# The first mixer's two attention loops: maxima ahead of the last unit's scale, values a step later, weight splits over two steps

## The chip, the cores and the metric

One core of one Trainium2 chip runs the whole kernel. The metric is the device time of one execution in microseconds (us). The core has five engines with a queue each: TensorE (PE) for matrix products and transposes, VectorE (DVE) and ScalarE (ACT) for work on elements, GpSimd (POOL), and SyncE (SP), which issues most of the transfers. Each queue is worked off in its order, and engines wait for one another through semaphores.

## What is computed

A trunk of two layers on 512 rows of 1024 numbers. The change lies in the attention part of the first layer, which has two kinds of heads behind one input projection; the rest (the gated feed-forward blocks and the second layer's attention) is not touched.

```python
def mla_attention(q_nope, q_rope, k_nope, k_rope, v):      # 8 heads
    s = (einsum(qn, k_nope) + einsum(qr, k_rope)) * scale  # 128 queries at a time
    s = where(kpos <= qpos, s, -inf)
    return einsum(softmax(s), v)

def diff_attention(q1, q2, k1, k2, v, lam, slopes):        # 4 heads
    p = softmax(q1 @ k1 * scale + bias) - lam * softmax(q2 @ k2 * scale + bias)
    return einsum(p, v)

o_mla = mla_attention(...)
o_diff = rms_norm(diff_attention(...), subln_g) * (1.0 - lam_init)
return concatenate([heads_last(o_mla), heads_last(o_diff)], -1) @ w_out
```

## The kernel before

The 512 rows are worked on as four tiles of 128. A product with weights is made of three matmuls (`mm3`, lines 263 to 265): every operand is split into a high part, rounded by a cast on ACT (`wh`, L72), and a low part, the difference, by a subtraction on DVE (`wl`, L73). `Weights` holds a list of weight units of 128x1024 numbers. `load` issues a unit's transfer into one of three raw buffers, `ahead(n)` casts and subtracts up to unit n, and `next` hands out the next unit.

The first attention (functions `m_...`) has 32 units: eight heads, in pairs, with four query tiles each. Unit i of a head has (i+1)*128 columns. A unit goes through these operations: the score product on PE into one of two banks (L776); the row maximum on DVE (L594, `softmax_negated`, which works on negated scores and also adds the mask); the exponential on ACT with its row sum (L596); reciprocal and scale on DVE (L782, L783, `m_scale`); the transposes on PE, i+1 of them (L793, `m_turn`); and the copy of the transposed weights out of the bank by DVE (L804) or, in the odd head, ACT (L802). After eight units the value product of a pair of heads follows (L811, `m_values`), and its split.

The second attention (functions `d_...`) has 16 units, four heads with query tiles 3, 2, 1, 0. A unit has two scores and two softmaxes (L674, L594, L596), a combination of the two on DVE (`d_combine`: reciprocals and products, L683 to L686), transposes (L868) and their copy (L870), the value product (L880), a scale by the first sum (L882), a square sum on ACT (L884), the root on POOL (`rstd`), and the norm on DVE (L890). After a head's four units `d_finish` transposes the head's output (L895) and splits it into `oD`, named odh and odl in the profile.

Between the steps of both loops PE gets other matmuls (`Fill`): the projections of values (`diff_v`, tile av) and of queries and keys (`diff_qk`, tile aqk) of the second attention, then the first half of the output product (`project`, tile ao). These are generators, and one call of `fill(n)` takes n pieces. Before, a piece is an `mm3`, so three matmuls.

Both loops stand in a manual schedule: the order in which the code issues the instructions is the order of each queue. In step n of the first loop the code issues the scale of unit n-1, the transposes and the copy of unit n-2, the score and the maximum of unit n, then one piece of filling. In step m of the second loop it issues the norm of unit m-3, the combination of m-1, the transposes and copy of m-2, scores and maxima of m, filling, the value product of m-2, and filling. In steps named in the table `made`, the cast and the subtraction of a weight unit follow at the end of the step.

The tiles that set limits: `s` (the weights of a unit) has four buffers, of which a unit of the second attention takes two; the banks of the matrix results are named a (three), s (two), t, o and n (one each). The first attention's transposes use t and n in turn, the second's use t.

Behind the loops come the second half of the output product, the residual and the first feed-forward block, in an order that is the same in both kernels.

Of the kernel before, what the change touches and what calls it, by code (L numbers as in the profile page):

```python
# [17 lines left out]
P = 128  # L18
# [68 lines left out]
def trunk(tc, A, out):  # L87
# [3 lines left out]
    with ExitStack() as top:  # L91
# [481 lines left out]
        def even():  # L573
            with ExitStack() as es:
# [24 lines left out]

                def diff_qk(h, z):  # L600
                    acc = bank("a", "aqk")
                    wh, wl = W.next()
                    for k in range(KD):
                        if k:
                            yield
                        mm3(acc, wh[:, k * P:(k + 1) * P], wl[:, k * P:(k + 1) * P],
                            xh[:, k], xl[:, k], k == 0, k == KD - 1)
                    if z == 0:
                        ACT.activation(dq[h], acc, AF.Copy, scale=-0.125)
                    else:  # L610
                        DVE.tensor_copy(dk[h], acc)

                def diff_v(tiles):
                    accs = [bank("a", "av") for _ in tiles]
                    for k in range(KD):
                        wh, wl = wv[k // 2]
                        c = slice((k % 2) * 512, (k % 2 + 1) * 512)
                        for a, i in zip(accs, tiles):
                            if k or i != tiles[0]:
                                yield  # L620
                            t = slice(i * P, (i + 1) * P)
                            mm3(a, xh[:, k, t], xl[:, k, t], wh[:, c], wl[:, c], k == 0, k == KD - 1)
# [3 lines left out]
                class Fill:  # L626
# [9 lines left out]
                    def end(self):  # L636
                        self(1000)

# [24 lines left out]
                otoks, dens, d_s, d_pt, d_r = {}, {}, {}, {}, {}  # L663
                D_UNITS = [(h, i) for h in range(4) for i in ORDER]

                def d_score(m):
                    h, i = D_UNITS[m]
                    w = (i + 1) * P
                    if i == ORDER[0]:
                        dens[h] = sx.tile([P, 6, NT], F32, tag="den", name="den", bufs=2)  # L670
                    s_ps = [bank("s", "sps") for _ in range(2)]
                    for z in range(2):
                        r = slice(z * 64, (z + 1) * 64)
                        PE.matmul(s_ps[z][:, :w], dq[h][r, i * P:(i + 1) * P], dk[h][r, :w], start=True, stop=True)  # L674
                    d_s[m] = [softmax_negated(s_ps[z][:, :w], alibi[h // 2][:, h % 2, 384 - i * P:], w)
                              for z in (1, 0)]

                def d_combine(m):
                    h, i = D_UNITS[m]
                    w = (i + 1) * P  # L680
                    (s2, st2), (s1, st1) = d_s[m]
                    v = dens[h][:, :, i:i + 1]
                    DVE.reciprocal(v[:, 0], st2[:, 1:2])  # L683
                    DVE.scalar_tensor_tensor(v[:, 1], v[:, 0], st1[:, 1:2], neglam[0], ALU.mult, ALU.mult)
                    DVE.scalar_tensor_tensor(s1[:, :w], s2[:, :w], v[:, 1], s1[:, :w], ALU.mult, ALU.add)
                    DVE.reciprocal(v[:, 2], st1[:, 1:2])  # L686
                    d_s[m] = s1

                with ExitStack() as e1:
# [82 lines left out]
                    def m_score(n):  # L772
                        p2, i, z = M_UNITS[n]
                        h, w = 2 * p2 + z, (i + 1) * P
                        s_ps = bank("s", "sps")
                        PE.matmul(s_ps[:, :w], mq[h][:, i * P:(i + 1) * P], mk[h][:, :w], start=True, stop=True)  # L776
                        m_s[n] = softmax_negated(s_ps[:, :w], dv[:, 0, 384 - i * P:], w)
# [7 lines left out]
                    def m_turn(n):  # L785
# [4 lines left out]
                        pt = pts[p2, z]  # L790
                        tp = bank("tn"[z], "tpp", 4, P)
                        for j in range(i + 1):
                            PE.transpose(tp[:, j], s[:, j * P:(j + 1) * P], ident[:])  # L793
                        for j in range(0, i + 1, 2):
# [23 lines left out]
                    made = {2: 14, 21: 15, 25: 16, 29: 17}  # L818
                    fill = Fill(diff_v((3, 2)), diff_v((1, 0)), *[diff_qk(h, z) for h in range(1, 4) for z in range(2)])
                    o = None  # L820
                    with tc.manual_schedule(engines=everything):
                        for n in range(M + 2):
                            if n + 2 in made:
                                W.load()
# [38 lines left out]
                def d_turn(m):  # L863
# [3 lines left out]
                    for j in range(i + 1):  # L867
                        PE.transpose(tp[:, j], s[:, j * P:(j + 1) * P], ident[:])  # L868
                    pt = sc.tile([P, 4, P], F32, tag="pt", name="pt", bufs=3)
# [3 lines left out]
                def d_value(m):  # L873
# [5 lines left out]
                    for j in range(i + 1):  # L879
                        PE.matmul(o[:], pt[:, j], dv[:, j, h * P:(h + 1) * P], start=(j == 0), stop=(j == i))  # L880
                    v, otok = dens[h][:, :, i:i + 1], otoks[h]
# [10 lines left out]
                def d_finish(h):  # L892
                    tp = bank("n" if h < 3 else "t", "tpo", NT, P)
# [9 lines left out]
                accs, wout = {}, {}  # L903

                def project(i, half, part):
# [6 lines left out]
                    for k in range(4):  # L912
                        if k:
                            yield
# [3 lines left out]
                        mm3(accs[i][half], o[0][:, k, q], o[1][:, k, q], wh[:, c], wl[:, c],  # L918
                            part == 0 and k == 0, part == 1 and k == 3)
# [4 lines left out]
                made = {3: (W, 18), 5: (W, 19), 6: (W2, 1), 7: (W, 20), 8: (W2, 2), 9: (W, 21), 10: (W2, 3),  # L924
                        11: (W, 22), 13: (W, 23), 15: (W, 24)}
                quota = [0, 0] + [5] * 2 + [4] * 8 + [3] * 4 + [4] * 3
                norms, turns = [], []
                with tc.manual_schedule(engines=everything):
                    W.ahead(17)
# [517 lines left out]
```

## Time and profile before

| what | before |
|---|---|
| median of three runs | 1194.86 us (1194.4 to 1195.18) |
| the profiled execution: time, span | 1195.44 us, 1193.6 us |
| busy in the span: PE, DVE, ACT, POOL | 1149.9, 815.0, 554.8, 55.4 us |
| mean granted clock of TensorE | 0.991 |
| instructions | 15204 |

The profile is of one execution. The span goes from its first to its last instruction; the execution's own time has 1.8 us around it. The granted clock is the share of full speed that TensorE was allowed. A row of the timeline gives the start, the duration, the engine, the line of the kernel and the operation with what it writes and reads; in brackets, how long the engine had been idle before it and what ended that. Records of matmuls overlap, since they are pipelined.

### The profile page before, as it was taken

How to read it: one execution, taken by the hardware profiler on the slowest of the kernel's cores; microseconds unless marked ns; L12 is line 12 of the kernel's file. 1: busy time of each engine (PE TensorE's matmuls, PEld its weight loads, DVE VectorE, ACT ScalarE, POOL GpSimd, SP SyncE). 2: the span in 40 equal slices, each digit the busy share in tenths (PEclk: the TensorE clock that was granted, in tenths of full speed). 3: DMA queues.
4: the chain of work that ended last, by engine and by line, in shares of the span. 5: the costliest groups of instructions: out<-in, count | busy, mean ns of one | idle time of the engine just before them, and what ended most of it. 6: DMA issues, size and time to landing. Idle time of an engine off the chain costs nothing. (4 is left out here: it accounts for less than half of the span.)

```text
span 1193.6 us, 15204 instructions
## 1 busy us (share of the span) xinstructions
PE 1149.9 (96%) x5668; PEld 939.8 (79%) x5668; DVE 815.0 (68%) x1431; ACT 554.8 (46%) x940; POOL 55.4 (5%) x139
## 2 busy tenths in 40 slices
PE   8987897899999999999999999999999999999997
PEld 7854575689888888888877888798988888888886
DVE  6655656556766657798984456566586666688996
ACT  5544444344434444455653255544454343445562
POOL 2100010120000000000020000001000000000002
PEclk9999999999999999999999999999999999999999
DMA  8410113115333233244645312212333333324461
GB/s 301 138 53 17 37 36 89 54 53 163 107 92 102 91 104 92 94 134 153 214 135 172 105 55 83 94 55 72 116 105 101 93 102 92 103 73 140 145 215 72
DMA packets 39194, 126.82 MB, mean 106 GB/s; under 512 B 4688, under 2 KB 6352, under 8 KB 39120
## 3 DMA queue, kind: packets, MB, share of 16 engines
q1 hardware_dynamic: 37056, 122.11, 32.6%
q10 hardware_dynamic: 2064, 3.74, 1.0%
q8 instruction: 45, 0.74, 0.3%
q14 instruction: 29, 0.24, 0.1%
HBM read 117.95 MB, written 6.29 MB: 104 GB/s over the span
## 5 line engine op out<-in xcount | busy, mean ns | idle before, releaser
L73 DVE TENSOR_TENSOR wl<-wraw,wh 128x1024 fp32r<-128x1024 f32 (+1 forms) x202 | 244.7, 1219 | 196.4 <-ACT wh L72 191.8
L72 ACT CAST wh<-wraw 128x1024 fp32r<-128x1024 f32 (+1 forms) x202 | 209.3, 1045 | 274.7 <-PE u L264 179.6
L264 PE MATMUL u<-xl,wh 128*128 128x512 f32 (+1 forms) x768 | 285.3, 372 | 0.1
L265 PE MATMUL u<-xh,wl 128*128 128x512 f32 (+1 forms) x768 | 285.2, 372 | 0.0
L263 PE MATMUL u<-xh,wh 128*128 128x512 f32 (+1 forms) x768 | 285.0, 372 | 0.2 <-ACT xh L171 0.2
L264 PEld LDWEIGHTS u<-xl,wh 128*128 128x128 f32 x768 | 144.7, 188 | 25.2 <-DVE xl L172 0.3
L263 PEld LDWEIGHTS u<-xh,wh 128*128 128x128 f32 x768 | 144.5, 188 | 25.4 <-ACT xh L171 0.6
L265 PEld LDWEIGHTS u<-xh,wl 128*128 128x128 f32 x768 | 144.7, 188 | 25.0
L264 PE MATMUL acc<-wl,gh 128*128 128x512 f32 (+1 forms) x250 | 96.9, 387 | 0.0
L265 PE MATMUL acc<-wh,gl 128*128 128x512 f32 (+1 forms) x250 | 96.8, 387 | 0.0
L263 PE MATMUL acc<-wh,gh 128*128 128x512 f32 (+1 forms) x250 | 96.8, 388 | 0.0
L596 ACT ACTIVATE s<-s,st 128x128 f32<-128x128 f32 (+3 forms) x64 | 35.7, 559 | 83.8 <-DVE st L594 83.8
L412 ACT ACTIVATE y<-u,cw 128x512 f32<-128x512 f32 x88 | 67.4, 774 | 1.7 <-PE u L265 1.7
L415 DVE SCALAR_TENSOR_TENSOR y<-u,cw,y 128x510 f32<-128x510 f32 x88 | 65.6, 747 | 2.5
L417 ACT ACTIVATE y<-y 128x512 f32<-128x512 f32 x44 | 27.7, 632 | 85.1 <-DVE y L415 85.0
L413 DVE SCALAR_TENSOR_TENSOR y<-u,cw,y 128x511 f32<-128x511 f32 x88 | 65.1, 744 | 0.9 <-ACT y L412 0.9
L263 PEld LDWEIGHTS acc<-wh,gh 128*128 128x128 f32 x250 | 46.9, 188 | 10.0 <-issue 0.6
L265 PEld LDWEIGHTS acc<-wh,gl 128*128 128x128 f32 x250 | 46.9, 188 | 9.7
L264 PEld LDWEIGHTS acc<-wl,gh 128*128 128x128 f32 x250 | 46.9, 188 | 9.6
L178 POOL TENSOR_TENSOR rv<-ms,epst 128x1 f32<-128x1 f32 x39 | 10.8, 278 | 924.9 <-ACT junk L230 846.8
L263 PE MATMUL apt<-xh,wh 128*128 128x512 f32 x128 | 51.4, 401 | 0.0
L264 PE MATMUL apt<-xl,wh 128*128 128x512 f32 x128 | 50.7, 396 | 0.0
(305 smaller groups left out, 1931.7 us busy)
## 6 DMA issues: line engine op xcount, KB each, us to landing
wraw<-in_ffn_w_up SPq DMA_DIRECT2D x88, 512.0 KB, 3.6
wraw<-in_ffn_w_down SPq DMA_DIRECT2D x44, 512.0 KB, 3.7
wraw<-in_od_w_dqk SPq DMA_DIRECT2D x12, 512.0 KB, 3.7
wraw<-in_ffn_w_down SPq DMA_DIRECT2D x22, 256.0 KB, 2.7
wraw<-in_ev_w_dqk SPq DMA_DIRECT2D x8, 512.0 KB, 3.7
wraw<-in_ev_w_out SPq DMA_DIRECT2D x8, 512.0 KB, 3.6
spill<-X SPq DMA_DIRECT2D x8, 512.0 KB, 2.6
X<-spill SPq DMA_DIRECT2D x8, 512.0 KB, 6.2
```

The costliest lines, as they stand in the source:

```text
L72: self.nc.scalar.copy(h[:, :w], raw[:, :w])
L73: self.nc.vector.tensor_tensor(l[:, :w], raw[:, :w], h[:, :w].bitcast(F32), ALU.subtract)
L178: POOL.tensor_tensor(v[:, :n], ms, epst[:, :n], ALU.add)
L263: PE.matmul(o, lh, rh, start=first, stop=False, skip_group_check=more)
L264: PE.matmul(o, lh, rl, start=False, stop=False, skip_group_check=more)
L265: PE.matmul(o, ll, rh, start=False, stop=last, skip_group_check=more)
L412: ACT.activation(y[:, z], u, AF.Identity, bias=c[:, 3:4], scale=c[:, 2:3])
L413: DVE.scalar_tensor_tensor(y[:, z, 1:], u[:, :S - 1], c[:, 1:2], y[:, z, 1:], ALU.mult, ALU.add)
L415: DVE.scalar_tensor_tensor(y[:, z, 2:], u[:, :S - 2], c[:, 0:1], y[:, z, 2:], ALU.mult, ALU.add)
L417: ACT.activation(y[:, 0], y[:, 0], AF.Silu)
L596: ACT.activation(s[:, :n], s[:, :n], AF.Exp, bias=st[:, 0:1], scale=-1.0, accum_out=st[:, 1:2])
```

## The change

In both loops the order of a step is written anew, and filling is cut into single matmuls (`one_by_one`). In the first loop the score of unit n+1 is issued in step n; the maximum of unit n (now `m_softmax`) comes ahead of the scale of unit n-1; the copies (`m_copy`) come behind the scale. In the second loop the score of unit m+1 is issued in the middle of step m; the transposes of m-2 and the value product of m-3 open the step; on DVE the maxima of m come first, then copy, output scale and combination. The norm is of m-4, and the loop has 18 steps for 17. The projection of one head's queries now stands between the two value projections. The weights' cast (`cast`) goes out at the end of a step and the subtraction (`rest`) in the next. The third `d_finish` uses bank t in place of n. The filling per step is set by two tables.

```diff
+                def one_by_one(o, lh, ll, rh, rl, first, last):
+                    if not first:
+                        yield
+                    PE.matmul(o, lh, rh, start=first, stop=False)
+                    yield
+                    PE.matmul(o, lh, rl, start=False, stop=False)
+                    yield
+                    PE.matmul(o, ll, rh, start=False, stop=last)
...
+                def cast(w):
+                    n = len(w.made)
+                    if len(w.raws) == n:
+                        w.load()
+                    h, l = w.pair()
+                    ACT.copy(h[:], w.raws[n][:])
+                    return w, h, l
+
+                def rest(w, h, l):
+                    n = len(w.made)
+                    DVE.tensor_tensor(l[:], w.raws[n][:], h[:].bitcast(F32), ALU.subtract)
+                    w.raws[n] = None
+                    w.made.append((h, l))
+                    if w is not W:
+                        wout[n] = w.next()
...
-                    made = {2: 14, 21: 15, 25: 16, 29: 17}
-                    fill = Fill(diff_v((3, 2)), diff_v((1, 0)), *[diff_qk(h, z) for h in range(1, 4) for z in range(2)])
+                    made = {9: 14, 27: 15, 30: 16}
+                    qk = [diff_qk(h, z) for h in range(1, 4) for z in range(2)]
+                    fill = Fill(diff_v((3, 2)), qk[0], diff_v((1, 0)), *qk[1:])
                         for n in range(M + 2):
...
-                            if 0 <= n - 1 < M:
+                            if n >= 2:
+                                tp = m_turn(n - 2)
+                                copy = lambda: m_copy(n - 2, tp)
+                            if n < M:
+                                m_softmax(n)
+                            else:
+                                d_softmax(m)
+                            if 1 <= n <= M:
                                 m_scale(n - 1)
+                            copy()
                             if m == 1:
                                 d_combine(0)
-                            if 0 <= n - 2 < M:
-                                m_turn(n - 2)
-                            if n < M:
-                                m_score(n)
-                            else:
-                                d_score(m)
+                            if n + 1 < M:
+                                m_score(n + 1)
                             if n % 8 == 2 and n > 8:
                                 o = m_values(n // 8 - 1)
-                            fill(1 if n < M else 3)
+                            fill((4, 4, 3, 3, 3, 3, 2, 2)[n % 8] if n < M - 8 else 4 if n < M else 12)
+                            if n + 1 >= M:
+                                d_score(m + 1)
                             if n % 8 == 3 and n > 8:
                                 split(oM[0][:, n // 8 - 1], oM[1][:, n // 8 - 1], o)
+                            if begun:
+                                rest(*begun)
+                                begun = None
                             if n in made:
-                                W.ahead(made[n])
+                                begun = cast(W)
...
-                    tp = bank("n" if h < 3 else "t", "tpo", NT, P)
+                    tp = bank("n" if h < 2 else "t", "tpo", NT, P)
...
-                quota = [0, 0] + [5] * 2 + [4] * 8 + [3] * 4 + [4] * 3
+                made = dict(zip((2, 3, 4, 5, 7, 8, 9, 11, 13, 15, 17), (W, W, W, W2, W2, W2, W, W, W, W, W)))
+                quota = [16] + [12] * 8 + [9, 8, 8, 9, 12, 8, 5, 4, 9]
...
+                    for m in range(2, N + 4):
+                        if m - 2 < N:
+                            tp = d_turn(m - 2)
+                        if 0 <= m - 3 < N:
+                            o = d_value(m - 3)
+                        if m < N:
+                            d_softmax(m)
+                        if m - 2 < N:
+                            d_copy(m - 2, tp)
+                        if 0 <= m - 3 < N:
+                            d_out(m - 3, o)
+                        if m - 1 < N:
+                            d_combine(m - 1)
+                        if begun:
+                            rest(*begun)
+                            begun = None
+                        n = quota[m - 2]
+                        fill((n + 1) // 2)
+                        if m + 1 < N:
+                            d_score(m + 1)
+                        fill(n // 2)
+                        if 0 <= m - 4 < N:
+                            d_norm(m - 4)
+                            if m == N + 3:
+                                fill.end()
+                            if (m - 4) % 4 == 3:
+                                d_finish((m - 4) // 4)
+                        if m in made:
+                            begun = cast(made[m])
```

Three places in the queues show what moved. First DVE, in the first loop, step 6 of the first pair of heads (the two ISA rows are the maximum and its read-out, 512 wide for unit 6; RECIPROCAL and TENSOR_SCALAR are the scale of unit 5; COPY is that of unit 4). Before:

```order
L782 RECIPROCAL st<-st 128x1
L783 TENSOR_SCALAR s<-s,st 128x384
L804 COPY pt<-tpp 128x2x128
L804 COPY pt<-tpp 128x128
L594 ISA s,st<-sps,dv 128x512
L594 ISA st 128x1
```

After:

```order
L594 ISA s,st<-sps,dv 128x512
L594 ISA st 128x1
L817 RECIPROCAL st<-st 128x1
L818 TENSOR_SCALAR s<-s,st 128x384
L843 COPY pt<-tpp 128x2x128
L843 COPY pt<-tpp 128x128
```

The maximum has moved from behind scale and copies to ahead of them.

Second PE, in the first loop at the second pair of heads (tpp are the transposes, sps the scores, av the filling matmuls). Before:

```order
L793 MATMUL tpp<-ident,s 128x128 x3
L776 MATMUL sps<-mk_150,mq_142 128x512
L263 MATMUL av<-wh,xh 128x512
L264 MATMUL av<-wl,xh 128x512
L265 MATMUL av<-wh,xl 128x512
```

After:

```order
L827 MATMUL tpp<-ident,s 128x128 x2
L807 MATMUL sps<-mk_150,mq_142 128x512
L608 MATMUL av<-wh,xl 128x512
L604 MATMUL av<-wh,xh 128x512
L606 MATMUL av<-wl,xh 128x512
L827 MATMUL tpp<-ident,s 128x128 x3
```

The score of 512 columns of this head (keys mk_150) stood behind the three transposes of the unit two before it; now it stands one step earlier, behind the two transposes of the unit ahead of that, and the three follow behind the filling.

Third DVE, in the second loop in the step of the second head's second unit (alibi is the table that the maximum adds, otok the head's output, den the reciprocals and factors of a unit). Before:

```order
L890 SCALAR_TENSOR_TENSOR otok_1447<-otok_1447,rr,small 128x128
L683 RECIPROCAL den<-st 128x1
L684 SCALAR_TENSOR_TENSOR den<-den,st,lam 128x1
L685 SCALAR_TENSOR_TENSOR s<-s,den 128x512
L686 RECIPROCAL den<-st 128x1
L870 COPY pt<-tpp 128x128
L594 ISA s,st<-sps,alibi 128x384
L594 ISA st 128x1
```

After:

```order
L594 ISA s,st<-sps,alibi 128x384
L594 ISA st 128x1
L928 COPY pt<-tpp 128x128
L944 TENSOR_SCALAR otok_1478<-o,den 128x128
L712 RECIPROCAL den<-st 128x1
L713 RECIPROCAL den<-st 128x1
L716 SCALAR_TENSOR_TENSOR den<-den,st,lam 128x1
L717 SCALAR_TENSOR_TENSOR s<-s,den 128x512
L658 TENSOR_TENSOR wl<-wraw,wh 128x1024
L952 SCALAR_TENSOR_TENSOR otok_1478<-otok_1478,rr,small 128x128
```

Maxima and copy have moved ahead of the combination, the output scale of the last value product stands between them, and the low part of a weight unit and the norm have moved behind the combination.

More of the change, by code (lines that the diff above doesn't have):

```diff
@@ L902, in even @@
                 BANK = {3: "aa", 2: "an", 1: "ss", 0: "aa"}
-                accs, wout = {}, {}
+                accs = {}
                 def project(i, half, part):
@@ L917, in project @@
                         wh, wl = wout[4 * part + k]
-                        mm3(accs[i][half], o[0][:, k, q], o[1][:, k, q], wh[:, c], wl[:, c],
-                            part == 0 and k == 0, part == 1 and k == 3)
+                        a = (accs[i][half], o[0][:, k, q], o[1][:, k, q], wh[:, c], wl[:, c])
+                        if part:
+                            mm3(*a, False, k == 3)
+                        else:
+                            yield from one_by_one(*a, k == 0, False)
                 N = len(D_UNITS)
```

94 lines of the change are left out of this document (47 added, 47 removed).

## The prediction

> **What bounds the kernel now.** I read the busy time by stretches first, to see where TensorE (PE) is not full; then the waits of that stretch; then the timeline of single steps there. The stretches below are the two interleaved attention loops, with the end of the program's span behind them (columns: stretch, length, busy time of PE, its weight loads, VectorE (DVE), ScalarE (ACT), GpSimd; granted clock; DMA).
>
> ```profile
> 63.69:239.71 176.02, 149.24 (x720) 100.64 (x719) 103.71 (x348) 74.97 (x221) 12.28 (x34) 0.97 0.16 49
> 240.00:1193.00 953.00, 941.46 (x4653) 787.23 (x4651) 671.86 (x1005) 444.56 (x650) 32.58 (x73) 1.00 0.36 110
> ```
>
> Behind 240 us PE is busy 941 of 953 us, and the change moves nothing there. Ahead of it PE lacks 26.8 of 176.0 us while DVE is busy for 104 and ACT for 75: no engine is full, so the engines wait for each other. The waits of the same stretch (us in total, times, longest) say how:
>
> ```profile
> ACT s L596 <- DVE st L594: 83.8, 48, 3.4
> DVE st L782 <- ACT s L596: 18.3, 25, 0.9
> DVE wl L73 <- ACT wh L72: 16.9, 10, 2.3
> PE tpp L793 <- DVE s L783: 15.3, 17, 2.4
> PE o L880 <- DVE pt L870: 9.8, 6, 2.6
> ```
>
> PE's idle time is nearly all in the last two: the first loop's transpose waits for the scale, the second's value product for the copy of the transposed weights. Both stand behind DVE, and DVE itself waits for ACT: for the exponential's sum, and for the cast that its weight subtraction needs. One step of the first loop in order of time (start, duration):
>
> ```profile
> 98.96 0.69 DVE L594 CUSTOM_DVE_ANT_0 s<-sps,dv 128x512 f32<-128x512 f32 x1
> ...
> 99.75 0.72 ACT L596 ACTIVATE s<-s,st 128x512 f32<-128x512 f32 x1 [1.00 <-DVE st L594]
> ...
> 100.60 0.16 DVE L782 RECIPROCAL st<-st 128x1 f32<-128x1 f32 x1 [0.34 <-ACT s L596]
> 100.80 0.49 DVE L783 TENSOR_SCALAR s<-s,st 128x512 f32<-128x512 f32 x1
> ...
> 101.43 0.63 PE L793 MATMUL tpp<-ident,s 128*128 128x128 f32 x4 [0.69 <-DVE s L783]
> 101.89 0.39 PE L776 MATMUL sps<-mk,mq 128*128 128x128 f32 x2
> ...
> 102.35 0.39 PE L264 MATMUL av<-wl,xh 128*128 128x512 f32 x1
> ...
> 102.58 0.40 PE L265 MATMUL av<-wh,xl 128*128 128x512 f32 x1
> ```
>
> Maximum, exponential, reciprocal, scale, transpose follow one another from 98.96 to 101.43, 2.5 us, and the maximum of the next unit stands behind this scale on DVE. So a step lasts as long as this circle, and PE's three filling matmuls are less than it. The bound here is that latency, not the work of an engine.
>
> **How much there is to win.** The stage begins and ends with these rows:
>
> ```profile
> 63.69 0.39 PE L776 MATMUL sps<-mk,mq 128*128 128x128 f32 x2
> ...
> 65.40 0.29 DVE L594 CUSTOM_DVE_ANT_0 s<-sps,dv 128x128 f32<-128x128 f32 x1
> ...
> 239.79 0.48 PE L263 MATMUL ao<-wh,odh 128*128 128x512 f32 x1
> 240.07 0.59 ACT L171 CAST odh<-tpo 128x512 fp32r<-128x512 f32 x1 [3.70 <-PE tpo L895]
> ...
> 240.69 0.69 DVE L172 TENSOR_TENSOR odl<-tpo,odh 128x512 fp32r<-128x512 f32 x1 [3.04 <-ACT odh L171]
> ```
>
> That is 176.1 us, from 63.69 to 239.79. PE's own work in it I price by starts, since its records overlap (0.39 long, 0.23 apart), from groups in which PE waits for nothing; the second filling matmul of a group (L264) starts 0.23 after the first really runs, so a group ends at that start less 0.23.
>
> ```profile
> 85.45 2.38 PE L811 MATMUL o<-pt,mv 128*64 128x512 f32 x16
> ...
> 88.09 0.40 PE L264 MATMUL av<-wl,xh 128*128 128x512 f32 x1
> ...
> 96.79 1.02 PE L776 MATMUL sps<-mk,mq 128*128 128x512 f32 x2
> ...
> 97.88 0.40 PE L264 MATMUL av<-wl,xh 128*128 128x512 f32 x1
> ...
> 141.55 1.13 PE L674 MATMUL sps<-dqk 64*128 64x512 f32 x4
> ...
> 142.95 0.39 PE L264 MATMUL aqk<-xl,wh 128*128 128x512 f32 x1
> ...
> 150.74 0.66 PE L868 MATMUL tpp<-ident,s 128*128 128x128 f32 x4
> ...
> 151.32 0.70 PE L674 MATMUL sps<-dqk 64*128 64x256 f32 x4
> ...
> 152.29 0.40 PE L264 MATMUL aqk<-xl,wh 128*128 128x512 f32 x1
> ...
> 154.13 1.05 PE L880 MATMUL o<-dv,pt 128*128 128x128 f32 x8
> ...
> 155.25 0.40 PE L264 MATMUL aqk<-xl,wh 128*128 128x512 f32 x1
> ```
>
> - Filling matmuls: 312 (projections 240, output products 72) x 0.23 = 71.8 us.
> - First loop's scores: 0.23 at width 128 (101.89 to 102.35 less 0.23), 0.86 at 512; the four widths average 0.545; 32 make 17.4. Its transposes: four in 0.46, so 80 make 9.2. Its four value products: 2.41 each, 9.6.
> - Second loop's score pairs: 1.17 at 512, 0.74 at 256, so 0.85 on average over the widths; 16 make 13.6. Transposes: four in 0.58, so 56 (40 and 16 of the finishes) make 8.1. Values: four in 0.89, so 40 make 8.9.
>
> The sum is 138.6 us. The stage takes 37.5 us more: 22 of it in the first loop (77.9 us to the row at 141.55, for 96 fills, the 32 scores, 76 transposes and three value products: 22.1 + 17.4 + 8.7 + 7.2 = 55.4), 15 in the second. The change adds and removes no matmul; 37.5 us is the most it can win here.
>
> **The change part by part.** *First loop.* The maximum of a unit now stands ahead of the last unit's scale, and its score is issued a step earlier. In a step DVE takes the maximum n while ACT still works on exponential n-1, then the scale n-1, then the copy n-2; the transpose n-2 comes a whole step after its scale. The latency of 2.5 us now spans two steps, and a step can be as short as the largest sum of one engine. Eight steps hold, on PE, scores 4.4, transposes 2.3, values 2.4 and 24 fills 5.5: 14.6 us, 1.8 a step. DVE would have 8 x (0.69 + 0.16 + 0.49) = 10.7 us and four copies if all eight were 512 wide, and they average 320; ACT has less than DVE. PE is the largest, so the circle's 19.5 us per eight steps falls towards 14.6. The fills (4,4,3,3,3,3,2,2) are small where the transposes and scores are large. What is late next: the first steps, where PE's third score needs the bank that the first maximum frees, and that maximum starts at 65.40 behind two weight subtractions, 0.7 us; I leave it standing.
>
> *Weights.* The cast goes out at the end of a step and the subtraction in the next. The subtraction costs what it did; what goes is DVE's standing behind ACT, the 16.9 us of ten waits.
>
> ```profile
> 186.26 1.22 DVE L73 TENSOR_TENSOR wl<-wraw,wh 128x1024 fp32r<-128x1024 f32 x1
> ...
> 188.45 0.67 DVE L594 CUSTOM_DVE_ANT_0 s<-sps,alibi 128x512 f32<-128x512 f32 x1
> ...
> 189.66 0.35 DVE L882 TENSOR_SCALAR otok<-o,den 128x128 f32<-128x128 f32 x1
> ...
> 193.35 0.16 DVE L683 RECIPROCAL den<-st 128x1 f32<-128x1 f32 x1
> ...
> 194.54 0.27 DVE L870 COPY pt<-tpp 128x128 f32<-128x128 f32 x1
> ```
>
> In a step of the second loop the 1.22 us stand behind the combine and ahead of the next maxima. Loads are issued in the same order on SP; a raw buffer is freed a step later, and three buffers keep the loads ahead by about three splits, some 8 us. I cost it at nothing.
>
> *Second loop.* The value product moves one step behind its transpose, so PE no longer waits for the copy (9.8 us); scores go out a step ahead. There is one step more (18 for 17), but it holds no more PE work. With twelve fills a step has on PE 2.76 + 0.36 + 0.56 + 0.85, and a quarter of a finish: 4.7 us. DVE's work in it is about 3.6 us:
>
> ```profile
> 141.50:211.00 69.50, 61.22 (x309) 42.98 (x307) 42.76 (x135) 32.51 (x93) 7.39 (x20) 0.98 0.18 54
> ```
>
> twelve units' maxima and what belongs to them fill 42.8 us of DVE there. Two new things bind. There are four buffers of s and a unit takes two, so the first maximum of unit m overwrites what the transpose of m-2 reads, and that transpose now opens the same step: transpose (0.3), two maxima (1.21 at 512), output scale (0.35), combine (1.19 at 512), in one line up to about 3.1 us before PE can begin the next transpose. Under a step of 4.7 us it is covered. In the last nine steps (4 to 12 fills, about 3.6 us a step at eight while scores last) it nearly shows, and so do DVE's 3.6: 1.5 us. And the third finish now takes the bank of the transposes: the next one waits for cast and subtraction (240.07 to 240.69, and 0.69): 1.5 us with the hand-overs.
>
> *Sum.* 138.6 + 0.7 + 1.5 + 1.5, and 3.8 us for edges of 52 steps that I can't place (below 0.1 each): 146.1 us for 176.1, **30 us** less. The profiled execution took 1195.44 us (span 1193.6), 0.6 above the median of 1194.86: 1165.4 for it, **1165 us** for the median.
>
> **The clock.** A part of the 37.5 us may be no wait at all:
>
> ```profile
> 70.00:80.00 10.00, 8.12 (x29) 5.34 (x30) 6.41 (x22) 3.65 (x13) 0.10 (x1) 0.83 0.19 54
> 110.00:120.00 10.00, 6.86 (x24) 3.90 (x24) 6.31 (x20) 3.85 (x10) 0.37 (x1) 0.88 0.19 52
> 180.00:190.00 10.00, 7.72 (x31) 5.60 (x32) 6.78 (x24) 3.42 (x11) 0.74 (x2) 0.83 0.33 87
> ```
>
> The granted clock falls to 0.83 to 0.88 in three of these stretches, all with PE busy under 8.2 of 10 us: together 4.6 us of full clock, part of it in idle time. With PE near full I expect no such dip. [...]
>
> **Rivals.**
> - *The dips stay.* Short waits remain in 52 steps. Against it: behind 240 us, with PE busy 99%, the row shows 1.00. Price up to 4.6 us: 1170.
> - *The second loop keeps its pace*, since transpose, maxima and combine stand in one line behind the four buffers, and DVE carries 3.6 us. For it: the last nine steps are hardly longer than that. Against: 4.7 us a step in the first half. If its 15 us stay and the first loop loses 19.5 of 22: 1175.
> - *Slower: the split weights come late.* PE runs in order, so a filling matmul whose low part isn't there holds the next transpose and score. If each of 14 splits (3 in the first loop, 11 in the second) held PE for a step, 3 x 1.8 + 11 x 4.7 = 57 us against 30: 1222. It decides from 2.1 us lateness each. Against it: in the new order the low part is made two steps or more ahead of its first use (the fourth output weight in step 10, used in 12).
> - *Nothing moves*: the circle goes on through a buffer or bank, and the new order only shifts it. Against it: the new order of DVE does put the maximum ahead of the scale, and two banks and four buffers serve the first loop's one score a step.
>
> **How the numbers follow.** Forecast 0.67; dips stay 0.08; second loop keeps its pace 0.17; nothing moves 0.04; slower 0.04. The low end is all 37.5 us won, 1157. The high end covers the second loop's case with a few us more, 1178; what lies outside is a fifth. Faster by over 0.2% (about what a measurement can tell from no change) holds the first three, 0.92.
>
> **What would show it.** Right: the stage from the first score to the first product with odh lasts 142 to 150 us; PE's wait of the transposes for the scale falls from 15.3 us to under 3, and that of the value product for its copy from 9.8 to near nothing; clock 1.00 through the stage; eight steps of the first loop in about 15 us. Wrong: PE waiting for wl, for a bank ("t" ahead of the fourth head's transposes by more than 2 us), or for the combine in each step of the second loop; or a longer time behind the stage, if the next weights come late.

## The result, and the profile after

The changed kernel takes **1159.87 us** (median of four runs, 1159.14 to 1161.31) where the kernel before took 1194.63 beside it: a ratio of **0.9713**, with a 95% interval of 0.9696 to 0.973, or 34.8 us less. The prediction had 1165 (1157 to 1178).

| what | before | after |
|---|---|---|
| profiled execution: time, span | 1195.44, 1193.6 us | 1159.68, 1157.9 us |
| the stage, from the first score to the first product with odh | 63.69 to 239.79, 176.1 us | 62.89 to 205.22, 142.3 us |
| of it up to the second loop's first score | 77.9 us | 58.2 us |
| mean granted clock | 0.991 | 0.998 |

The first part holds 96 filling matmuls before and 104 after, and four transposes fewer, so it compares to within some 1.4 us.

The busy time by stretches of the kernel after, for the stage and for what lies behind it (columns as in the prediction: stretch, length, PE, weight loads, DVE, ACT, GpSimd, granted clock, DMA; the cut between the two lies 0.02 us behind the stage's end):

```profile
62.89:205.24 142.35, 140.15 (x722) 98.74 (x720) 102.02 (x348) 75.38 (x221) 19.12 (x34) 1.00 0.18 57
205.24:1157.90 952.66, 940.54 (x4655) 786.12 (x4652) 671.71 (x1005) 444.50 (x650) 32.00 (x73) 1.00 0.35 111
```

PE lacks 2.2 us in the stage where it lacked 26.8. DVE and ACT do what they did (102 and 75 us), in a shorter time. Behind the stage there are 952.7 us, against 953.9 before. All waits of PE in the stage are three (us in total, times, longest):

```profile
PE tpp L922 <- DVE odl L172: 1.4, 1, 1.4
PE sps L807 <- DVE st L594: 0.5, 1, 0.5
PE sps L697 <- DVE st L594: 0.2, 1, 0.2
```

The 15.3 us of the transposes behind the scale and the 9.8 us of the value products behind the copy are gone. The other engines' waits in the same stage show what DVE and ACT have left:

```profile
ACT s L596 <- DVE st L594: 23.2, 19, 3.0
ACT s L596 <- DVE st L817: 16.4, 20, 1.7
...
DVE s L594 <- PE tpp L922: 3.5, 5, 1.0
...
DVE st L817 <- ACT s L596: 0.3, 1, 0.3
...
DVE wl L658 <- ACT wh L653: 0.3, 1, 0.3
```

ACT still waits for the maximum, but that now costs nobody anything: DVE's wait for the exponential's sum fell from 18.3 us to 0.3, and its wait for the casts of weights from 16.9 us to 0.3. A step of the first loop in the timeline (start, duration), and behind it the score with which the next eight steps begin:

```profile
86.69 0.69 DVE L594 CUSTOM_DVE_ANT_0 s<-sps,dv 128x512 f32<-128x512 f32 x1 [0.21 <-PE sps L807]
...
87.48 0.72 ACT L596 ACTIVATE s<-s,st 128x512 f32<-128x512 f32 x1 [0.48 <-DVE st L817]
...
88.56 0.69 DVE L594 CUSTOM_DVE_ANT_0 s<-sps,dv 128x512 f32<-128x512 f32 x1
...
89.15 0.39 PE L807 MATMUL sps<-mk,mq 128*128 128x128 f32 x2
89.17 0.16 DVE L817 RECIPROCAL st<-st 128x1 f32<-128x1 f32 x1
89.37 0.49 DVE L818 TENSOR_SCALAR s<-s,st 128x512 f32<-128x512 f32 x1
...
90.00 0.63 PE L827 MATMUL tpp<-ident,s 128*128 128x128 f32 x4
...
103.90 0.39 PE L807 MATMUL sps<-mk,mq 128*128 128x128 f32 x2
```

From a unit's maximum (86.69) over its exponential (87.48) to its scale (89.37) and transposes (90.00) go 3.3 us, more than the 2.5 us before. But the next unit's maximum (88.56) stands inside that time, and by the scale the score after it (89.15) is issued. The latency got longer and no longer sets the step: eight steps take 103.90 - 89.15 = 14.75 us. What PE still loses is the start and the third finish:

```profile
64.95 0.70 PE L807 MATMUL sps<-mk,mq 128*128 128x256 f32 x2 [0.51 <-DVE st L594]
...
194.87 0.60 PE L957 MATMUL tpo<-ident,otok 128*128 128x128 f32 x4
...
195.50 0.59 ACT L171 CAST odh<-tpo 128x512 fp32r<-128x512 f32 x1 [2.34 <-PE tpo L957]
...
196.12 0.69 DVE L172 TENSOR_TENSOR odl<-tpo,odh 128x512 fp32r<-128x512 f32 x1 [2.37 <-ACT odh L171]
...
196.87 0.44 PE L922 MATMUL tpp<-ident,s 128*128 128x128 f32 x2 [1.40 <-DVE odl L172]
```

The third score waits 0.51 us for the bank that the first maximum frees. The transposes behind the third finish wait 1.40 us until cast and subtraction have emptied bank t.

### The profile page after: what moved, and what is told of

Same layout as the page of the kernel before. It is cut to its first block, busy times and chain, and to the rows that moved or that the text cites. A ratio compares the mean times of both kernels' runs of the same rounds, so it can differ in the third digit from the quotient of the medians.

```text
span 1157.9 us, 15198 instructions
## 1 busy us (share of the span) xinstructions
PE 1139.7 (98%) x5668; PEld 936.2 (81%) x5668; DVE 813.0 (70%) x1431; ACT 555.1 (48%) x940; POOL 61.8 (5%) x139
## 4 chain that ended last, share of the span: by engine, by line
PE 45%; issue 2%; DVE 1%; POOL 1%; ACT 1%; POOLq 0%; DVEq 0%; ACTq 0%
PE u L264 7%; PE u L265 7%; PE u L263 7%; PE acc L263 3%; PE acc L264 3%; PE acc L265 3%; PE apt L263 3%; PE apt L264 3%; PE apt L265 3%; PE cp L1182 1%; PE apv L263 1%; PE apv L265 1%; PE apv L264 1%; PE o L1266 1%; PE o L1343 1%
## 5 line engine op out<-in xcount | busy, mean ns | idle before, releaser
L73 DVE TENSOR_TENSOR wl<-wraw,wh 128x1024 fp32r<-128x1024 f32 (+1 forms) x189 | 228.8, 1218 | 179.0 <-ACT wh L72 178.6
L72 ACT CAST wh<-wraw 128x1024 fp32r<-128x1024 f32 (+1 forms) x189 | 195.8, 1046 | 273.1 <-PE u L264 179.7
```

The source lines that it names most:

```text
L72: self.nc.scalar.copy(h[:, :w], raw[:, :w])
L73: self.nc.vector.tensor_tensor(l[:, :w], raw[:, :w], h[:, :w].bitcast(F32), ALU.subtract)
```

## The experiments

Ten kernels, each timed in turn with the kernel before. Except where it is said otherwise, an edit is made to the kernel after, and differences are to its 1159.87 us. Every kernel here computes the whole of the function; only orders, places, the filling per step and one bank differ. The kernel before, beside them, took 1195.43 to 1196.57 us where it took 1194.63 beside the kernel after, so a difference of times is good to about 2 us; the ratios allow for that. "First" and "second" are the parts of the stage up to the second loop's first score and from there to the first product with odh, in the profiled execution; in the kernel after they are 58.2 and 84.1 us. What lies outside the stage differs too, though its code is the same: the profiled execution of the kernel after has no stretch at half clock there but the one with which every trace ends, while that of the kernel before and that of each experiment has one or two (most near 12 us, some near 660). So up to 2 us of a difference between profiled executions (4 with the even filling) lie outside the stage that the edits touch.

| kernel | median, us | ratio to before (95%) | first, second, us |
|---|---|---|---|
| first loop in the old order | 1174.37 | 0.9827 (0.981 to 0.9843) | 71.4, 83.8 |
| scale ahead of the maximum | 1167.01 | 0.9757 (0.9739 to 0.9775) | 63.3, 84.7 |
| score in the same step | 1178.43 | 0.9858 (0.9843 to 0.9872) | 77.0, 83.8 |
| second loop in the old order | 1170.37 | 0.9789 (0.9774 to 0.9803) | 58.3, 93.6 |
| splits in one step | 1172.78 | 0.9817 (0.9804 to 0.983) | 59.1, 93.7 |
| even filling | 1162.7 | 0.9731 (0.9717 to 0.9744) | 57.9, 84.1 |
| third finish on bank s | 1159.19 | 0.9705 (0.9692 to 0.9718) | 58.2, 82.8 |
| second softmax first | 1161.52 | 0.972 (0.9707 to 0.9733) | 58.3, 84.1 |
| both loops in the old order | 1182.39 | 0.9881 (0.9866 to 0.9896) | 71.4, 90.9 |
| the same, splits in one step | 1194.9 | 0.9988 (0.9974 to 1.0002) | 75.7, 98.7 |

### The first loop in the old order

```diff
+                            if 1 <= n <= M:
+                                m_scale(n - 1)
...
                             if n >= 2:
-                                tp = m_turn(n - 2)
-                                copy = lambda: m_copy(n - 2, tp)
+                                m_copy(n - 2, m_turn(n - 2))
                             if n < M:
+                                m_score(n)
                                 m_softmax(n)
...
-                            if n + 1 < M:
-                                m_score(n + 1)
...
-                            fill((4, 4, 3, 3, 3, 3, 2, 2)[n % 8] if n < M - 8 else 4 if n < M else 12)
+                            fill(3 if n < M - 8 else 4 if n < M else 12)
```

> The changed kernel with the first loop's step in the old order (scale and copy ahead of the maximum, score in the unit's own step, three fills a step); second loop, weight splits and single fills as changed. Theory (the circle of maximum, exponential, scale is what bound the first loop): the loop goes back from 58 to about 77 us, so 1178 to 1182 us in all, and PE's waits of the transposes for the scale return to 12 to 18 us. Rival (finer filling and the weight splits over two steps brought the gain): under 1168.

It is 14.5 us slower, and nearly all of it (13.2) lies in the first loop. The waits for the scale are back:

```profile
PE tpp L827 <- DVE s L818: 10.3, 19, 1.1
...
DVE st L817 <- ACT s L596: 19.6, 26, 0.9
```

The mechanism is the one expected, the sizes aren't: 1174.37 us stand against 1178 to 1182, and the wait of 10.3 us against 12 to 18. I had thought that this loop would be as long as before (77.9), and it is 71.4. Of the 19.7 us that the changed first loop wins, 6.5 do not come from its order. The last two kernels say where most of that is from.

### Maximum and score, each by itself

First kernel: only the scale of unit n-1 stands ahead of the maximum of unit n again, and the score stays a step early.

```diff
-                            if n < M:
-                                m_softmax(n)
-                            else:
-                                d_softmax(m)
                             if 1 <= n <= M:
                                 m_scale(n - 1)
+                            if n < M:
+                                m_softmax(n)
+                            else:
+                                d_softmax(m)
```

> One swap in the first loop of the changed kernel: the scale of the last unit ahead of this unit's maximum; scores stay a step ahead. Theory (the order on DVE closes the circle again: maximum, exponential, reciprocal, scale, next maximum; by the rows about 1.3, 1.7, 2.0 and 2.3 us a step at the four widths, 14.4 for eight steps and DVE's copies beside it, against PE's 14.6): both bounds nearly equal, so 4 to 10 us slower than the changed kernel, 1164 to 1170. Rival (the maximum ahead of the scale is the whole gain): 1175 or more. Second rival (scores a step earlier are the whole gain): 1161 or less.

Second kernel: the maximum stays ahead of the scale, and the score of unit n is issued in step n, just ahead of it.

```diff
                             if n < M:
+                                m_score(n)
                                 m_softmax(n)
...
-                            if n + 1 < M:
-                                m_score(n + 1)
```

> The changed kernel with the score of a unit issued in the unit's own step, ahead of its maximum, in the first loop; the maximum stays ahead of the scale. Theory (the step then holds transpose, score, maximum, scale in one line, 2.5 us at width 512 for 1.7 of PE work): 3 us more per eight steps, 10 to 14 us in all, 1170 to 1174. Rival (the early score is not needed once the maximum is ahead of the scale): under 1163.

The first costs 7.1 us, as expected. The second costs 18.6 us, more than expected, and also more than the kernel in which both parts are undone (14.5). Its waits say why:

```profile
PE tpp L827 <- DVE s L818: 14.0, 24, 1.0
...
DVE s L594 <- PE sps L807: 29.4, 26, 2.9
```

DVE's maximum waits for a score 26 times, 29.4 us in all (3.1 us in the kernel after), and the scale of the unit before stands behind that waiting maximum, though its own operands are there (the exponential before it has ended ahead of the maximum in all 26). So a maximum ahead of the scale is worth something only where its score lies ready: with the early score it brings 7.1 us. Without it the kernel is 4.1 us slower than the one with the first loop in the old order, in which the copies stand ahead of the maximum as well and the filling is even. The early score alone, with the maximum behind the scale and copies and filling as in the kernel after, already brings 7.4 us (1174.37 to 1167.01).

### The second loop in the old order

The order in the loop is that of before (norm, combination, transposes and copy, scores, maxima, filling, value product and finish); the splits over two steps stay. The filling per step goes back to that of before as well, in single matmuls.

```diff
-                    for m in range(2, N + 4):
+                    for m in range(2, N + 3):
...
                         if m - 1 < N:
                             d_combine(m - 1)
+                        if m - 2 < N:
+                            d_copy(m - 2, d_turn(m - 2))
+                        if 2 < m < N:
+                            d_score(m)
+                        if m < N:
+                            d_softmax(m)
...
+                        if m - 2 < N:
+                            d_out(m - 2, d_value(m - 2))
```

> The changed kernel with the second loop's step in the old order (value product in the step of its transposes, score of unit m in step m, norm, combination and copy ahead of the maxima); first loop and weight splits as changed. Theory (the value's wait for its copy and the combination's wait for the exponential bind there): 11 to 15 us slower than the changed kernel, 1171 to 1175, with 7 us or more of PE waiting for pt. Rival (second loop was helped by the fill table alone): under 1164.

10.5 us slower, a little less than expected, nearly all in the second loop. In the profiled execution the clock stands at half there for 6.8 us, which is up to 3.4 of the 9.5 us by which the loop is longer. The value product waits for its copy again, 4.1 us for the product itself and 6.6 us for its weight loads, which in part are the same time. DVE itself stands ahead of the norm that opens the step:

```profile
PE o L938 <- DVE pt L928: 4.1, 3, 1.5
...
PEld o L938 <- DVE pt L928: 6.6, 6, 1.9
...
DVE otok L952 <- ACT wh L653: 13.5, 9, 1.8
...
DVE otok L952 <- POOL rr L181: 5.7, 4, 1.4
```

That is 19.2 us in 13 waits, of which the kernel after has 0.5. The norm needs POOL's root, and combination, copy and maxima stand behind it; the cast that the view names for nine of them ends 0.02 us after the norm has started, so it is not what they wait for. The value product moved a step and the norm moved behind the combination in one change, and no run parts the two.

### The weights' cast and subtraction in one step

```diff
                             if n in made:
-                                begun = cast(W)
+                                rest(*cast(W))
...
                         if m in made:
-                            begun = cast(made[m])
+                            rest(*cast(made[m]))
```

> The changed kernel with the low part of a weight unit made at the end of the step of its cast, in place of the next step. Theory (DVE stands behind ACT's cast for 1 to 2 us fourteen times, of which PE's steps of 4.7 us cover most, while the steps of 3.6 us do not): 2 to 7 us slower than the changed kernel, 1162 to 1167. Rival (the splits over two steps carry much of the gain): 1172 or more. Second rival (they do nothing): within 1 us of 1160.

12.9 us slower: the rival held. 0.9 us of it lies in the first loop, which has three splits, and 9.6 in the second, which has eleven; there the clock stands at half for 3.4 us, which is up to 1.7 of them. The other 2 us are outside the stage.

```profile
PE sps L697 <- DVE st L594: 5.7, 4, 1.7
...
DVE wl L658 <- ACT wh L653: 9.3, 11, 3.5
...
DVE wo L658 <- ACT wo L653: 2.9, 1, 2.9
```

The subtraction waits in DVE's queue for a cast that ACT has not finished, for 12.2 us in all (9.3 of it in the four waits that begin before the cast does), and the maxima of the next step stand behind it. PE then waits for the bank that those maxima free.

### Even filling, bank s, and the order of the two softmaxes

```diff
-                            fill((4, 4, 3, 3, 3, 3, 2, 2)[n % 8] if n < M - 8 else 4 if n < M else 12)
+                            fill(3 if n < M - 8 else 4 if n < M else 12)
```

> The changed kernel with three fills in each of the first 24 steps, in place of 4,4,3,3,3,3,2,2. Theory (PE is full whatever the fills of a step, and everything it waits for is a step away): 0 to 2 us slower, 1160 to 1162. Rival (the fill's distribution is what keeps PE full): 1165 or more.

The time is 2.8 us longer, and 0.7 above the range expected, but the stage is as long as in the kernel after (142.0 us). It begins at 65.0 us for 62.9: ahead of it the clock stood at half for 6.8 us, of which the profile of the kernel after shows nothing. Behind it there are 2.0 us more, with one such stretch of 3.4 us. The table of fillings is worth nothing that these runs could show.

```diff
-                    tp = bank("n" if h < 2 else "t", "tpo", NT, P)
+                    tp = bank("n" if h < 2 else "s" if h == 2 else "t", "tpo", NT, P)
```

> The changed kernel with the third finish in a score bank, which is free by then, in place of the bank of the transposes. Theory (the next transposes wait for that bank, 1.4 us in the trace): PE's wait for odl goes and the stage is 1 to 1.5 us shorter, 1158 to 1159, at the edge of what the timing tells. Rival (the output product's third tile, which uses the score banks next, waits in its place): no change.

The wait of 1.40 us for bank t is gone (0.4 us of another stands in its place), the stage is 141.0 us, 1.3 less, and the time is 0.7 us less, which the interval does not tell from none. So the 1.4 us was the price of that bank.

```diff
-                              for z in (0, 1)]
+                              for z in (1, 0)]
...
-                    (s1, st1), (s2, st2) = d_s[m]
+                    (s2, st2), (s1, st1) = d_s[m]
```

> The changed kernel with the maximum of the second softmax ahead of the first's, so that the first maximum of a unit overwrites a buffer that the combination read and no transpose. Theory (the four buffers hold DVE, 3.5 us in the trace, but PE's step covers it): within 1 us of the changed kernel, 1159 to 1161. Rival (the four buffers set the second loop's step): 2 us or more faster, under 1158.

The stage is unchanged (142.4 us); the 1.7 us by which the time is longer, 0.5 beyond the range expected, lie outside it. DVE's wait behind the transposes is unchanged as well. In the kernel after it stands here, behind the first maximum of the step and the transposes of the unit two before:

```profile
146.13 0.55 DVE L594 CUSTOM_DVE_ANT_0 s<-sps,alibi 128x384 f32<-128x384 f32 x1
...
147.36 0.28 PE L922 MATMUL tpp<-ident,s 128*128 128x128 f32 x1
...
147.67 0.56 DVE L594 CUSTOM_DVE_ANT_0 s<-sps,alibi 128x384 f32<-128x384 f32 x1 [0.98 <-PE tpp L922]
```

and in the experiment here:

```profile
148.71 0.56 DVE L594 CUSTOM_DVE_ANT_0 s<-sps,alibi 128x384 f32<-128x384 f32 x1 [0.98 <-PE tpp L922]
```

It is the second maximum of the step in both, not the first, and it waits as long as before. The first one starts 1.2 us ahead of the transposes, so it cannot overwrite what they read, in the kernel after either. The edit thus did not move the wait, and says little of its rival. What speaks against the rival is that no wait of PE follows from this wait of DVE. Which buffer is behind it stays open.

### Both loops old, with and without the split over two steps

The first of these kernels has both old orders from above. The second one has in addition cast and subtraction in one step; of the change it keeps only the filling in single matmuls, the moved projection of queries, the steps at which weights are loaded and split, the order of the two softmaxes and of their reciprocals, and the third finish's bank.

> Both loops in the old order of before; the weights' cast and subtraction over two steps, and the filling in single matmuls, stay as in the changed kernel. Theory (the two loops' gains are independent, each loop a bound of its own): 1159.9 + 14.5 + 10.5 = 1184.9, so 1182 to 1188; first loop 71.4 us, second 93.6, stage 165. Rival (one loop gives back what the other gained): 1190 or more, or 1178 or less.

> As the kernel with both loops in the old order, but each weight unit's cast and subtraction stand in one step again, so that of the change only the single matmuls of the filling, the moved first query projection and the steps of the splits are left. Theory (standing behind the cast costs DVE the same in the old order): 8 to 13 us more than with the split over two steps, so 1192 to 1198, as before's 1195. Rival (the split over two steps counts only in the new order, where the score and its maximum open the step): within 3 us of the other kernel, 1182 to 1188, and what is missing up to before's 1195 is the single matmuls' doing.

The first lies in the range of its theory, at its low end, with both parts of the stage about as in the kernels with one loop old (71.4 for 71.4, 90.9 for 93.6, of which up to 3.4 were half clock). The ratios to before are 0.9881 and 0.9988. The last one can't be told from 1, so what it keeps brings nothing by itself that these runs could tell. Whether the new orders need the filling in single matmuls no run shows. Between the two lie 12.8 us (0.0107 of 1195), as in the new order (12.9): the split is worth the same in both, and its rival fell. The two orders about add up too: the four ratios 0.9988, 0.9881, 0.9789, 0.9713 give 12.8 us for the splits, then 11.0 for the first loop, then 9.1 for the second; taken out of the kernel after one at a time, they were 12.9, 14.5 and 10.5. The two orders together come to 20.1 us by the ratios and 22.5 by the times, for 25.0 one at a time, which the intervals do not tell apart. In the waits of the kernel with splits in one step stands what it costs:

```profile
PE tpp L827 <- DVE s L818: 13.9, 19, 2.4
PE o L933 <- DVE pt L923: 7.7, 7, 2.2
PE tpo L952 <- DVE otok L947: 2.6, 1, 2.6
...
DVE wl L658 <- ACT wh L653: 20.7, 13, 2.4
```

With the split over two steps the same waits of PE are 10.3 us (longest 1.1), 4.8 (1.5) and 1.4, and no subtraction of weights waits for its cast. With the longer waits the clock is lower as well. In the kernel with splits in one step a stretch at half clock begins at 172.37 us, 0.85 us behind the end of a wait of 1.98 us:

```profile
169.15 0.40 PE L606 MATMUL aqk<-xl,wh 128*128 128x512 f32 x1
171.52 0.49 PE L933 MATMUL o<-dv,pt 128*128 128x128 f32 x2 [1.98 <-DVE pt L923]
```

```profile
170.00:180.00 10.00, 8.48 (x40) 6.58 (x41) 6.19 (x23) 5.09 (x15) 1.18 (x4) 0.83 0.34 105
```

and the same ten us of the kernel with splits over two steps, at the full clock with no more of PE's time busy:

```profile
170.00:180.00 10.00, 8.53 (x44) 5.96 (x43) 6.89 (x25) 4.37 (x16) 1.48 (x4) 1.00 0.14 52
```

Three stretches of 3.4 us at half clock begin in the stage of the one (at 138.23, 172.37 and 237.22 us, so the last lies in it for 1.0 us), none in that of the other. That is up to 3.9 of the 12.0 us by which the two stages differ in the profiled executions (174.35 and 162.34), and PE's waits, 26.5 us for 18.6 in all, are 7.9 more.

## Why the prediction was right, step by step

- **The bound** was named rightly: latencies, not an engine's work. The floor of 138.6 us for PE's own work stood: the stage came to 142.3, and nothing in ten experiments went under 141.0.
- **First loop.** Eight steps of 14.6 us were forecast, 14.75 came. Of the two parts that the prediction named, the score a step earlier brings 7.4 us by itself; the maximum ahead of the scale brings 7.1 us with it, and nothing without it. The loop lost 19.7 us, as forecast (19.5), but its order is worth only 11 to 14.5 of them; the prediction gave the order all. With the old order another 4.3 are the weights' (75.7 to 71.4 between the last two kernels); with the new one their share of this loop is 0.9.
- **Second loop.** The value product's wait went, and the second loop fell from 98.2 to 84.1 us. The order is worth 9 to 10.5 us, near the 9.8 us of that wait, but in part by luck: with this loop alone in the old order the wait is only 4.1 us, up to 3.4 us are half clock, and the norm at the head of the step, which the prediction does not speak of, holds DVE for 19.2 us. The rival in which it keeps its pace fell. The line behind the four buffers of s was read wrongly, since the first maximum overwrites nothing that the transposes read, and overrated: DVE waits there for 3.5 us in all, and PE not at all; the 1.5 us for the last nine steps did not come.
- **Weights.** "I cost it at nothing" was right as a cost and wrong as an account. The prediction saw DVE's 16.9 us behind the cast go, and gave that no share of the gain, since PE's waits carried other names. Moved to the next step, the subtraction is worth 12.8 us in either order, over a third of the gain. The sum came out because it was made from PE's floor and not from the parts; that the sizes of the parts were off did not reach it. The rival with late low parts fell: PE waits for no wl.
- **What stays.** 0.7 us for the start was 0.51, 1.5 for the third finish 1.40 (and the kernel on bank s shows that bank to be its cause). The 3.8 us for edges of 52 steps was the term that was mis-sized: 142.3 less 138.6 is 3.7 for everything together, so with 2.1 in the three waits some 1.6 are left for it. This and the last nine steps are 3.7 us; the other 2 us of the 5.7 by which the profiled execution lay below its forecast of 1165.4 are outside the stage (it begins 0.8 us earlier and 1.2 us less follow it). They look like luck: the profile of the kernel before has stretches at half clock at 11.74 and 684.16 us and that of the kernel after has neither, while nine of the ten experiments, with the same code there, have one near 12 us.
- **The clock.** No dip in the stage, as forecast, in the stretches that answer to those at 0.83, 0.88 and 0.83:

```profile
70.00:80.00 10.00, 10.00 (x52) 6.97 (x52) 7.95 (x30) 5.91 (x18) 0.10 (x1) 1.00 0.01 2
...
110.00:120.00 10.00, 10.00 (x52) 6.87 (x48) 6.60 (x21) 5.35 (x13) 0.00 (x0) 1.00 0.15 52
...
180.00:190.00 10.00, 9.81 (x52) 6.59 (x51) 9.16 (x33) 7.95 (x23) 2.06 (x4) 1.00 0.15 53
```

  The rival in which the dips stay fell. Short waits, which it names, brought none: the kernel with the score in the same step has 24 waits of PE of at most 1.0 us for the scale, 14 us in all, and the clock stays at 1.00 through its stage. The three dips before begin 0.45 to 1.30 us behind single waits of 1.93 to 2.57 us; in the stage after, the longest wait is 1.40 us. The three stretches at half clock in the stage before are up to 5.1 of the 33.8 us by which it got shorter.

## What to carry to other kernels

Before reordering, price the floor of the engine that should be full, from the starts of its own groups; a forecast made from that floor survives a wrong account of which edit brings what. In queues that run in order, an operation moved ahead of another gains only if its own operand is already there: move the producer a step earlier first, or the move can cost time, as it did here (4.1 us). And look for pairs such as cast and subtraction that stand next to each other on two engines: the second one's wait appears under other names further down, so a step between them can be worth as much as the reorder that one is looking at (12.8 us here, for 11.0 and 9.1 of the two loops' orders).

## What the runs showed of the hardware beside that

Apart from the one with which every trace ends (within the span 4.3 us of it in the kernel before, 4.1 in the kernel after), the stretches at half clock are 3.41 us long, or twice that, in every trace here. In the kernel before they begin at 11.74, 73.18, 117.55, 182.41 and 684.16 us, so three of them lie in the stage. PE has five waits of more than 1.9 us there:

| wait of PE, us | ends at, us | waits for | next stretch at half clock |
|---|---|---|---|
| 2.36 | 71.88 | the scale, L783 | at 73.18, 1.30 us later |
| 1.93 | 117.10 | the scale, L783 | at 117.55, 0.45 us later |
| 1.92 | 138.23 | the scale, L783 | none for 44 us |
| 2.57 | 181.87 | the copy, L870 | at 182.41, 0.54 us later |
| 2.57 | 207.04 | the copy, L870 | none in the stage |

The value product's two waits among them, the last two of the table, are alike:

```profile
181.87 1.19 PE L880 MATMUL o<-dv,pt 128*128 128x128 f32 x6 [2.57 <-DVE pt L870]
...
207.04 0.94 PE L880 MATMUL o<-dv,pt 128*128 128x128 f32 x6 [2.57 <-DVE pt L870]
```

Behind the first the clock falls, behind the second it stays. So in this trace the length of a wait does not tell whether a dip follows, and these rows do not show what does. A dip can follow a shorter wait too: in the kernel with only the splits in one step, the one dip of the stage begins at 193.3 us, 2.3 us behind the end of PE's longest wait there, which is 1.68 us.
